# The first matrix of both MLPs by seven block products for the latent tokens, its feature sums made beside the norm

## The chip, the cores and the metric

The kernel runs on 1 core of a Trainium2 chip. The metric is the device time of one execution in microseconds. The core has a matrix engine (PE, with weight loads shown as PEld), a vector engine (DVE), an engine for activations (ACT), a general one (POOL) and SP, which here issues all DMA transfers.

## The reference

One inference step of a backbone of two layers with 1280 tokens: 1024 latent ones and 256 prompt ones, 1024 features each. After a mixer (DeltaNet and attention in the first layer, a gated recurrence in the second) every layer has an MLP with 4096 hidden features:

```
def sq_relu_mlp(h, w1, w2):
    return jnp.square(jax.nn.relu(h @ w1)) @ w2
...
yp = yp + (mp[5] * sq_relu_mlp(modulate(yp, norm2_g[l], mp[3], mp[4]), ff_w1[l], ff_w2[l])).astype(yp.dtype)
ys = ys + (ms[5] * sq_relu_mlp(modulate(ys, norm2_g[l], ms[3], ms[4]), ff_w1[l], ff_w2[l])).astype(ys.dtype)
```

`modulate` is an RMS norm over the features, times a scale per feature, plus a shift per feature. `p` stands for the prompt tokens and `s` for the latent ones; everything is float32.

## The kernel before

Features lie on the partitions, in eight chunks of 128; tokens lie along the free dimension in three groups (`TT`, line 24): group 0 and group 1 are 512 latent tokens each, group 2 is the 256 prompt tokens. Each float32 operand of a large matmul is split into a high part (a cast to the matmul type, on ACT) and a low part (the rest, subtracted on DVE or POOL), and each product is three matmuls (high by high, high by low, low by high; `gemm_tile`, lines 463 to 468). `wload` (439) loads a chunk of weights through raw slots (`wraw`, four of them in the MLPs), and keeps high and low parts in one of four weight slots.

The work around the change runs in this order in each layer.

- `OutProj.finish` (689) multiplies the mixer's result by the output projection, adds it to x (`evac`, line 702, on DVE) and calls `step` after each of the eight output chunks of a token group. First come chunks 0 to 3 for all groups, then chunks 4 to 7 of group 0, of group 1, of group 2. x stays in SBUF in three tiles, `x0` to `x2`.
- `norm_steps` (736) builds the norm into these steps. `Norm.square` (387) squares a chunk on ACT (line 396) and lets PE add up the chunk before it (`flush`, line 332). `stat` (398) turns the sums into 1/rms per token; `apply` (409) scales the chunks on DVE (418), makes the high part on ACT (419) and the low part on DVE (421) or POOL (427). Group 0's `stat` and `apply` are called at steps 4 and 5 of group 1, group 1's at steps 4 and 6 of group 2, and group 2's are left to the first pair of ff1. The squares and the scaled chunks share four scratch slots (`t0` in `ffr`, `t1` in `tt`, two each).
- `ff1` (491) goes over 16 pairs `p` of hidden chunks. For each token group and each chunk of the pair it runs 8 x 3 matmuls, a relu on ACT (506) and a square on DVE (507). Then POOL makes four differences of the hidden blocks (511), and the hidden features and the differences go to DRAM (`Dh`, `Dt`, lines 513 and 514).
- `ff2` (517) goes over eight groups of four hidden chunks. It has the second matrix for the latent tokens as seven block products of a 2 x 2 scheme, from those differences and from sums of weights that POOL makes, and adds each to x (`acc`, line 526).

No order is written out: the framework's planner, at build time, puts the instructions of each engine in order by its own estimates of their costs, and takes among those that are ready the one that comes first in the program. The profile shows matmuls of ff1 between those of OutProj, for instance. At run time each engine keeps to the order it was given.

## Time and profile before

| what | us |
|---|---|
| median of 3 runs | 3238.04 (3234.08 to 3239.82) |
| the profiled execution | 3233.86 |
| its span, first to last instruction | 3232.1 |
| PE busy in the span | 3060.8 |
| DVE, ACT, POOL busy | 1864.1, 1209.4, 1117.5 |

PE's matmuls overlap, so a row's duration (0.39 us for 512 columns) is longer than the distance from one to the next; the rate is read from start to start. Of the stages that the change touches, ff1 runs from some 1092 to 1525 us in the first layer and from some 2397 to 2830 us in the second, each followed by ff2. A wait names the instruction that released the waiting one.

### The profile page before, as it was taken

The page shows a single profiled execution, that of the slowest core. Times are in us where ns is not written, and L with a number is a line of the kernel's source. Part 1 is how long each engine was busy: PE and PEld are TensorE (multiplying, and loading weights), DVE is VectorE, ACT ScalarE, POOL GpSimd, SP SyncE. Part 2 cuts the span into 40 slices and gives each one's busy share as a digit, 9 for nine tenths or more (in the row PEclk, how much of TensorE's full clock was granted, in tenths as well). Part 3 has the DMA queues.
Part 4 walks back from the last instruction along what each step waited for, and adds up shares of the span by engine and source line. Part 5 has one row for each costly group of instructions (what it writes and reads, how often), then busy time and mean ns, then how long its engine had stood idle before and what let it go on. Part 6 is the DMA issues. An engine that isn't in the chain of part 4 may idle for free.

```text
span 3232.1 us, 50272 instructions
## 1 busy us (share of the span) xinstructions
PE 3060.8 (95%) x19927; PEld 2485.3 (77%) x19927; DVE 1864.1 (58%) x2952; ACT 1209.4 (37%) x1972; POOL 1117.5 (35%) x781
## 2 busy tenths in 40 slices
PE   8989975889989999999999998999899999999999
PEld 5776764565557788888888877888678888888888
DVE  5548887576751522223777766888352222277776
ACT  5555433454331411112333335878241111133332
POOL 0000004454531432334767641000133333287664
PEclk9999986999999999999999998999999999999999
DMA  5346677536871233334534230110313333454332
GB/s 205 85 142 175 172 180 188 156 124 208 245 239 52 69 127 127 127 127 170 181 110 157 84 106 24 37 45 25 108 46 139 120 123 119 153 191 149 128 107 85
DMA packets 274058, 416.53 MB, mean 129 GB/s; under 512 B 77210, under 2 KB 139450, under 8 KB 269726
## 3 DMA queue, kind: packets, MB, share of 16 engines
q1 hardware_dynamic: 273822, 413.31, 40.0%
q8 instruction: 157, 2.57, 0.3%
q14 instruction: 79, 0.65, 0.1%
HBM read 290.80 MB, written 122.41 MB: 128 GB/s over the span
## 4 chain that ended last, share of the span: by engine, by line
PE 74%; DVE 8%; DMA 3%; issue 3%; ACT 2%; POOL 2%; SPq 1%; DVEq 0%; POOLq 0%; ACTq 0%
PE ps_mm L467 14%; PE ps_mm L466 14%; PE ps_mm L468 13%; PE ps_w L546 4%; PE ps_w L547 4%; PE ps_w L548 4%; PE ps_mm L547 4%; PE ps_mm L548 4%; PE ps_mm L546 4%; DVE prod L1600 2%; PE ps_ad L300 2%; PE ps_w L1959 1%; DVE Vinv L1601 1%; PE ps_w L1955 1%; PE ps_s L1918 1%
## 5 line engine op out<-in xcount | busy, mean ns | idle before, releaser
L466 PE MATMUL ps_mm<-hhi,whi 128*128 128x512 f32 (+2 forms) x2768 | 991.0, 359 | 24.7 <-ACT hhi L686 13.5
L467 PE MATMUL ps_mm<-hlo,whi 128*128 128x512 f32 (+2 forms) x2768 | 990.2, 358 | 8.8 <-POOL hlo L427 8.8
L468 PE MATMUL ps_mm<-hhi,wlo 128*128 128x512 f32 (+2 forms) x2768 | 987.6, 357 | 1.6 <-POOL wlo L457 1.6
L466 PEld LDWEIGHTS ps_mm<-hhi,whi 128*128 128x128 f32 (+1 forms) x2768 | 525.8, 190 | 111.1 <-ACT hhi L686 13.9
L467 PEld LDWEIGHTS ps_mm<-hlo,whi 128*128 128x128 f32 (+1 forms) x2768 | 526.2, 190 | 90.7 <-POOL hlo L427 11.6
L468 PEld LDWEIGHTS ps_mm<-hhi,wlo 128*128 128x128 f32 (+1 forms) x2768 | 526.3, 190 | 81.8 <-issue 6.0
L507 DVE TENSOR_TENSOR hid<-ffr 128x512 f32<-128x512 f32 (+1 forms) x192 | 148.9, 777 | 589.3 <-ACT ffr L506 507.1
L536 POOL TENSOR_TENSOR wlo<-ar,whi 128x1024 fp32r<-128x1024 f32 x96 | 246.7, 2584 | 268.7 <-ACT whi L535 251.2
L506 ACT ACTIVATE ffr<-ps_mm 128x512 f32<-128x512 f32 (+1 forms) x192 | 100.6, 525 | 548.2 <-PE ps_mm L468 546.5
L526 DVE SCALAR_TENSOR_TENSOR x<-ps_mm,mod,x 128x512 f32<-128x512 f32 x272 | 200.4, 746 | 82.8 <-PE ps_mm L548 82.6
L526 DVE SCALAR_TENSOR_TENSOR x<-ps_w,mod,x 128x512 f32<-128x512 f32 (+1 forms) x304 | 185.6, 632 | 100.7 <-PE ps_w L548 100.5
L511 POOL TENSOR_TENSOR tt<-hid 128x512 f32<-128x512 f32 x64 | 83.3, 1301 | 414.0 <-DVE hid L507 414.0
L453 ACT CAST whi<-wraw 128x512 fp32r<-128x512 f32 (+1 forms) x237 | 136.7, 617 | 197.9 <-PE ps_mm L467 84.1
L535 ACT CAST whi<-ar 128x1024 fp32r<-128x1024 f32 x96 | 98.0, 1051 | 292.6 <-PE ps_w L547 208.3
L457 POOL TENSOR_TENSOR wlo<-wraw,whi 128x512 fp32r<-128x512 f32 (+1 forms) x93 | 139.1, 1515 | 186.1 <-DVE hlo L687 93.0
L828 POOL MEMSET pad<- 128x2 f32 (+2 forms) x60 | 3.9, 119 | 439.8 <-DVE xc L846 200.0
L457 DVE TENSOR_TENSOR wlo<-wraw,whi 128x512 fp32r<-128x512 f32 x144 | 136.2, 972 | 33.2 <-ACT whi L453 33.0
L546 PE MATMUL ps_w<-pp,whi 128*128 128x256 f32 x512 | 143.6, 283 | 4.6 <-DVE x L526 4.6
L547 PE MATMUL ps_w<-pp,whi 128*128 128x256 f32 x512 | 143.4, 283 | 0.0
L548 PE MATMUL ps_w<-pp,wlo 128*128 128x256 f32 x512 | 141.0, 283 | 0.0
L511 POOL TENSOR_TENSOR tt<-hid,tt 128x512 f32<-128x512 f32 x64 | 85.3, 1333 | 118.2 <-DVE hid L507 118.0
L702 DVE SCALAR_TENSOR_TENSOR x<-ps_mm,mod,x 128x512 f32<-128x512 f32 (+1 forms) x40 | 25.9, 655 | 150.3 <-PE ps_mm L468 138.5
(416 smaller groups left out, 5890.1 us busy)
## 6 DMA issues: line engine op xcount, KB each, us to landing
...
wraw<-ff SPq DMA_DIRECT2D x128, 256.0 KB
...
br<-dh SPq DMA_DIRECT2D x128, 256.0 KB
ar<-ff SPq DMA_DIRECT2D x128, 256.0 KB
br<-dt SPq DMA_DIRECT2D x128, 256.0 KB
...
```

The lines of the kernel that those rows point to most:

```text
L453: nc.scalar.copy(hv[:, o:o + half], raw[:, :half])
L457: e.tensor_tensor(lv[:, o:o + half], raw[:, :half], hv[:, o:o + half], op=ALU.subtract)
L466: nc.tensor.matmul(ps, whi[:, k, :], hhi[:, k, :], start=first and k == k0, stop=False)
L467: nc.tensor.matmul(ps, whi[:, k, :], hlo[:, k, :], start=False, stop=False)
L468: nc.tensor.matmul(ps, wlo[:, k, :], hhi[:, k, :], start=False, stop=last and k == k1 - 1)
L507: nc.vector.tensor_tensor(hid[i][:, t0:t0 + tw], r[:, :tw], r[:, :tw], op=ALU.mult)
L511: nc.gpsimd.tensor_tensor(t[:, j], x, y, op=ALU.subtract)
L526: nc.vector.scalar_tensor_tensor(xt[ti][:, o, :], ps[:, :tw], Gt[:, o, cc:cc + 1], xt[ti][:, o, :], op0=ALU.mult, op1=ALU.add)
L536: nc.gpsimd.tensor_tensor(lo[:, c], s, hi[:, c], op=ALU.subtract)
L546: nc.tensor.matmul(ps, ah, bh, start=first, stop=False, skip_group_check=True)
L547: nc.tensor.matmul(ps, ah, bl, start=False, stop=False, skip_group_check=True)
L548: nc.tensor.matmul(ps, al, bh, start=False, stop=last, skip_group_check=True)
```

## The change

For the two groups of latent tokens, a pair of hidden chunks and the two halves of the input features are taken as a 2 x 2 by 2 x 2 block product, made with seven products in place of eight. A product is four feature chunks by three matmuls of 512 columns. The weight sums are made for every pair on POOL, in place, in the raw tiles; their high and low parts take four weight slots per pair instead of two. The feature sums (blocks 2, 3 and 4) are made once per layer, while group 1 is normed; they take the SBUF of the x tiles, so x is stored to DRAM (`Dxm`) during OutProj and loaded again at the start of ff2. The norm of the latent groups now scales x in place, without scratch. Group 2 (prompt) keeps its 2 x 8 x 3 matmuls of 256 columns per pair. The four differences of hidden blocks are made on DVE and stored one by one. All norms send the last chunk's sum to PE in `square` instead of in `stat`, and their scratch is one set of four slots (`ffr`). In ff2, half of the feature blocks take a tile `t4` in place of a second `tt`.

```diff
-        if k == KC - 1 and self.late:
-            self.sq = self.g.cp.tile([128, 512], F32, tag="nsq", name="nsq", bufs=1)[:, :self.tw]
-        else:
-            self.sq = self.al("t%d" % (k % 2))[:, :self.tw]
+        self.sq = self.al("t%d" % (k % 2))[:, :self.tw]
         self.g.nc.scalar.activation(self.sq, self.x[:, k, :], AF.Square)
+        if k == KC - 1:
+            self.flush(k)
     def stat(self):
         g, nc, nch = self.g, self.g.nc, self.nch
-        self.flush(KC - 1)
...
+class NormBlocks(Norm):
+    def scaled(self, k, pb, At):
+        x = self.x[:, k, :]
+        self.g.nc.vector.scalar_tensor_tensor(x, x, At[:, k, 0:1], pb, op0=ALU.mult, op1=ALU.mult)
+        return x
+    def biased(self, hi, lo, t, sh):
+        self.g.nc.scalar.activation(hi, t, AF.Identity, bias=sh)
+        self.g.nc.vector.scalar_tensor_tensor(lo, t, sh, hi, op0=ALU.add, op1=ALU.subtract)
+    def plain(self, hi, lo, t):
+        self.g.nc.scalar.copy(hi, t)
+        self.g.nc.gpsimd.tensor_tensor(lo, t, hi, op=ALU.subtract)
+    def apply(self, At, Bt, hhi, hlo):
+        if self.ti == 2:
+            Norm.apply(self, At, Bt, hhi, hlo)
+            self.last_block()
+            return
+        g, nc, com = self.g, self.g.nc, self.com
+        pb = self.rows()
+        hi, lo = hhi[self.ti], hlo[self.ti]
+        if self.ti == 0:
+            for k in range(KC):
+                self.biased(hi[:, k, :], lo[:, k, :], self.scaled(k, pb, At), Bt[:, k, 0:1])
+            com["x0"] = self.x
+            return
+        dsh = g.cp.tile([128, 4], F32, tag="dsh", name="dsh", bufs=1)
+        nc.vector.tensor_tensor(dsh, Bt[:, 4:8, 0], Bt[:, 0:4, 0], op=ALU.subtract)
+        d2, d3 = [[g.fp.tile([128, 2, 512], F32, tag="hid", name="nd", bufs=4) for i in range(2)] for _ in range(2)]
+        com["d4"] = g.fp.tile([128, 4, 512], F32, tag="tt", name="nd4", bufs=1)
+        x0 = com["x0"]
+        for k in range(4):
+            u, v = self.scaled(k, pb, At), self.scaled(4 + k, pb, At)
+            t, e2, e3 = x0[:, k, :], d2[k // 2][:, k % 2], d3[k // 2][:, k % 2]
+            nc.vector.tensor_tensor(t, u, t, op=ALU.subtract)
+            nc.vector.tensor_tensor(e2, v, t, op=ALU.subtract)
+            nc.gpsimd.tensor_tensor(e3, v, u, op=ALU.subtract)
+            nc.gpsimd.tensor_tensor(com["d4"][:, k], x0[:, 4 + k, :], e2, op=ALU.subtract)
+            self.plain(hi[:, k, :], lo[:, k, :], t)
+            self.biased(hi[:, 4 + k, :], lo[:, 4 + k, :], v, Bt[:, 4 + k, 0:1])
+        for n, (d, tag) in enumerate(((d2, "x0"), (d3, "x1"))):
+            t = g.xm.tile([128, 2, 4, 512], F32R, tag=tag, name=f"tb{2 + n}", bufs=1)
+            for k in range(4):
+                self.biased(t[:, 0, k], t[:, 1, k], d[k // 2][:, k % 2], Bt[:, 4 + k, 0:1] if n == 0 else dsh[:, k:k + 1])
+            com[2 + n] = (t[:, 0], t[:, 1])
+    def last_block(self):
+        g, com = self.g, self.com
+        hi = g.xm.tile([128, 4, 512], F32R, tag="x2", name="tb4h", bufs=1)
+        lo = g.fp.tile([128, 4, 512], F32R, tag="t4", name="tb4l", bufs=1)
+        for k in range(4):
+            self.plain(hi[:, k], lo[:, k], com["d4"][:, k])
+        com[4] = (hi, lo)
...
-def ff(g, l, xt, hhi, hlo, Gt, pend, after):
+def ff(g, l, Dxm, h, com, Gt, pend, after):
     Dh = g.dp.tile([NFC // 2, 128, 2, T], F32, name=f"dh{l}")
     Dt = g.dp.tile([NFC // 2, 128, 4, 512], F32, name=f"dt{l}")
-    ff1(g, l, hhi, hlo, pend, Dh, Dt)
-    ff2(g, l, xt, Gt, after, Dh, Dt)
+    ff1(g, l, h, com, pend, Dh, Dt)
+    xt = [xtile(g, ti) for ti in range(3)]
+    ff2(g, l, xt, Dxm, Gt, lambda o, ti: after(o, ti, xt[ti]), Dh, Dt)
...
+def three(g, ps, a, b, first, last):
+    (ah, al), (bh, bl) = a, b
+    g.nc.tensor.matmul(ps, ah, bh, start=first, stop=False, skip_group_check=True)
+    g.nc.tensor.matmul(ps, ah, bl, start=False, stop=False, skip_group_check=True)
+    g.nc.tensor.matmul(ps, al, bh, start=False, stop=last, skip_group_check=True)
+def wslot(g):
+    w, i = g.wslots[g.nw % len(g.wslots)]
+    g.nw += 1
+    return [w.tile([128, KC, 128], F32R, tag=n + str(i), name=n).rearrange("p k c -> p (k c)") for n in ("whi", "wlo")]
...
+def ff1(g, l, h, com, pend, Dh, Dt):
+    def product(ps, w, half, b, first):
+        for k in range(4):
+            c = slice(512 * half + 128 * k, 512 * half + 128 * k + 128)
+            three(g, ps, [v[:, c] for v in w], [v[:, k, :] for v in b], first and k == 0, k == 3)
+    def saved(ps):
+        t = scratch()
+        nc.scalar.copy(t, ps)
+        return t
+    def square(out, ps):
+        r = scratch()[:, :out.shape[-1]]
+        nc.scalar.activation(r, ps, AF.Relu)
+        nc.vector.tensor_tensor(out, r, r, op=ALU.mult)
+    def add_square(out, t, ps):
+        nc.vector.tensor_tensor(out, t, ps, op=ALU.add)
+        nc.vector.scalar_tensor_tensor(out, out, 0.0, out, op0=ALU.max, op1=ALU.mult)
+    def sum_(out, x, y, op=ALU.subtract):
+        nc.gpsimd.tensor_tensor(out, x, y, op=op)
+    def parts(srcs, e):
+        hi, lo = wslot(g)
+        for j, s in enumerate(srcs):
+            c = slice(512 * j, 512 * j + 512)
+            nc.scalar.copy(hi[:, c], s)
+            e.tensor_tensor(lo[:, c], s, hi[:, c], op=ALU.subtract)
+        return hi, lo
...
+        if p % 2:
+            t = pool.tile([128, 2, 2, 512], F32, tag="tt", name="raw", bufs=1)
+            raw = [[t[:, i, j] for j in range(2)] for i in range(2)]
+        else:
+            raw = [[wraw(g) for j in range(2)] for i in range(2)]
+            for j in range(2):
+                nc.sync.dma_start(raw[i][j], g.A["ff1"][l, 2 * p + i][:, 512 * j:512 * j + 512])
+        (a11, a12), (a21, a22) = raw
+        w1, w2 = parts((a11, a12), nc.gpsimd), parts((a21, a22), nc.vector)
+        sum_(a22, a21, a22, ALU.add)
+        sum_(a21, a11, a21)
+        sum_(a11, a22, a11)
+        sum_(a12, a12, a11)
+        s12, s34 = parts((a22, a11), nc.vector), parts((a21, a12), nc.gpsimd)
+        hid = [pool.tile([128, 1024], F32, tag="hid", name="hid", bufs=4) for i in range(2)]
+        hp = [pool.tile([128, 256], F32, tag="hidp", name="hidp", bufs=2) for i in range(2)]
+        (b11, b12), (b21, b22) = [[t[:, 0:512], t[:, 512:1024]] for t in hid]
+        def prompt(i, w):
+            ps = bank(g, "w")[:, :256]
+            for k in range(KC):
+                three(g, ps, [v[:, 128 * k:128 * k + 128] for v in w], (hhi[2][:, k, :], hlo[2][:, k, :]), k == 0, k == KC - 1)
+            square(hp[i], ps)
+        def late():
+            if pend:
+                pend.pop(0)()
+        ca = bank(g, "mm")
+        product(ca, w1, 0, part(0, 0), True)
+        late()
+        t = saved(ca)
+        ps = bank(g, "w")
+        product(ps, w1, 1, part(0, 4), True)
+        late()
+        add_square(b11, t, ps)
+        if p:
+            prompt(0, w1)
+        product(ca, s12, 1, com[2], False)
+        u1 = saved(ca)
+        cb = bank(g, "w")
+        product(cb, s12, 0, part(1, 0), True)
+        product(ca, s34, 0, com[3], False)
+        u2 = saved(ca)
+        add_square(b22, u2, cb)
+        if not p:
+            prompt(0, w1)
+        prompt(1, w2)
+        product(ca, w2, 1, com[4], False)
+        square(b21, ca)
+        product(cb, s34, 1, part(1, 4), False)
+        add_square(b12, u1, cb)
+        ts = []
+        for j, (x, y) in enumerate(((b12, b11), (b22, 0), (b22, b12), (b21, 1))):
+            ts.append(scratch())
+            nc.vector.tensor_tensor(ts[j], x, ts[y] if j % 2 else y, op=ALU.subtract)
+            nc.sync.dma_start(Dt[p, :, j], ts[j])
+        for i in range(2):
+            nc.sync.dma_start(Dh[p, :, i, 0:NL], hid[i])
+            nc.sync.dma_start(Dh[p, :, i, NL:], hp[i])
...
         chain = [bank(g, "mm") for m in range(4)]
         load_w(0)
         a11, b11 = weights([ar[:, 0]]), feats(block_of(0, 0))
+        if gi == 0:
+            load_x(g, xt[0], xsrc, 0)
...
+        if gi == 0:
+            load_x(g, xt[2], xsrc, 2)
         prompt((a11, a12), 0)
...
         w, f = weights(s2), feats(comb(2))
+        if gi == 0:
+            load_x(g, xt[1], xsrc, 1)
         for m in range(4):
...
-            return g.fp.tile([128, T], F32R, tag="hid", name="ndg", bufs=4)
-        return g.fp.tile([128, 512], F32, tag={"t0": "ffr", "t1": "tt"}[tag], name="n" + tag, bufs=2)
+            return g.fp.tile([128, 1024], F32R, tag="hid", name="ndg", bufs=4)
+        return g.fp.tile([128, 512], F32, tag="ffr", name="n" + tag, bufs=4)
...
-    step, left, h = norm_steps(g, (At, Bt), ff_scratch(g), {1: 4, 2: 4}, {1: 5, 2: 6})
-    xt = op.finish(cut, g.mod[l][:, 16:24, :], step)
-    ff(g, l, xt, *h["h"], Gt, left, lambda o, ti: after(o, ti, xt[ti]))
+    com = {}
+    Dxm = g.dp.tile([128, KC, T], F32, name=f"dxm{l}")
+    step, left, h = norm_steps(g, (At, Bt), ff_scratch(g), {1: 4, 2: 4}, {1: 5, 2: 6}, com=com)
+    def keep(o, ti, x):
+        step(o, ti, x)
+        if o % 4 == 3:
+            t0, tw = TT[ti]
+            nc.sync.dma_start(Dxm[:, o - 3:o + 1, t0:t0 + tw], x[:, o - 3:o + 1, :])
+    op.finish(cut, g.mod[l][:, 16:24, :], keep)
+    ff(g, l, Dxm, h["h"], com, Gt, left, after)
```

## Rows read from the trace of the kernel before

**Rows 1.** The page of the profile, its start and part 1, whole span.

```profile
span 3232.1 us, 50272 instructions
...
PE 3060.8 (95%) x19927; PEld 2485.3 (77%) x19927; DVE 1864.1 (58%) x2952; ACT 1209.4 (37%) x1972; POOL 1117.5 (35%) x781
```

**Rows 2.** Busy time by stretch: ff1 of both layers, ff2 of the first.

```profile
core 0: us, PE busy (x) PEld busy (x) DVE busy (x) ACT busy (x) POOL busy (x), PEclk, DMA share, GB/s
1092.00:1525.00 433.00, 431.89 (x2261) 372.59 (x2261) 125.76 (x147) 89.74 (x171) 138.31 (x101) 1.00 0.36 126
2397.00:2830.00 433.00, 431.89 (x2263) 372.65 (x2263) 125.44 (x147) 89.15 (x170) 139.26 (x101) 1.00 0.36 126
1600.00:1800.00 200.00, 200.00 (x1065) 173.34 (x1065) 148.08 (x178) 65.26 (x72) 133.75 (x70) 1.00 0.38 127
```

**Rows 3.** Timeline of PE, one pair: start us, us, engine, line, operation.

```profile
1302.75 0.40 PE L466 MATMUL ps_mm<-hhi,whi 128*128 128x512 f32 x1
...
1324.54 0.28 PE L466 MATMUL ps_mm<-hhi,whi 128*128 128x256 f32 x1
...
1330.29 0.40 PE L466 MATMUL ps_mm<-hhi,whi 128*128 128x512 f32 x1
```

**Rows 4.** Groups by line and shape inside ff1: count | busy, mean ns | idle before.

```profile
L457 POOL TENSOR_TENSOR wlo<-wraw,whi 128x512 fp32r<-128x512 f32 x28 | 44.1, 1594 | 0.0
...
L511 POOL TENSOR_TENSOR tt<-hid 128x512 f32<-128x512 f32 x30 | 38.8, 1295 | 206.4 <-DVE hid L507 206.4
L507 DVE TENSOR_TENSOR hid<-ffr 128x512 f32<-128x512 f32 x56 | 38.8, 692 | 229.8 <-ACT ffr L506 195.8 <-issue 34.0
L457 DVE TENSOR_TENSOR wlo<-wraw,whi 128x512 fp32r<-128x512 f32 x28 | 37.1, 1364 | 9.5 <-ACT whi L453 9.5
L506 ACT ACTIVATE ffr<-ps_mm 128x512 f32<-128x512 f32 x56 | 33.5, 598 | 256.3 <-PE ps_mm L468 256.3
L453 ACT CAST whi<-wraw 128x512 fp32r<-128x512 f32 x56 | 32.0, 618 | 52.4 <-POOL tt L511 26.4 <-PE ps_mm L467 25.9
```

**Rows 5.** Timeline of DVE from OutProj to ff1, first layer (columns as rows 3).

```profile
1056.98 0.75 DVE L702 SCALAR_TENSOR_TENSOR x<-ps_mm,mod,x 128x512 f32<-128x512 f32 x1 [1.33 <-PE ps_mm L468]
1059.48 0.75 DVE L418 SCALAR_TENSOR_TENSOR nt<-x,A,ps_w 128x512 f32<-128x512 f32 x1 [1.75 <-PE ps_w L369]
...
1072.97 0.47 DVE L702 SCALAR_TENSOR_TENSOR x<-ps_mm,mod,x 128x256 f32<-128x256 f32 x1
...
1081.30 0.16 DVE L403 TENSOR_SCALAR nst<-ps_w 128x4 f32<-128x4 f32 x1 [4.93 <-PE ps_w L347]
...
1084.89 1.41 DVE L418 SCALAR_TENSOR_TENSOR nt<-x,A,ps_w 128x512 f32<-128x512 f32 x2 [1.12 <-PE ps_w L369]
```

**Rows 6.** Waits of PE, 960 to 1120 us: total us, times, longest.

```profile
PE ps_mm L466 <- ACT hhi L419: 2.7, 2, 1.6
PE ps_mm L467 <- POOL hlo L427: 2.3, 1, 2.3
PE ps_w L368 <- DVE ndg L361: 0.9, 1, 0.9
```

**Rows 7.** Busy time by stretch after those waits (columns as rows 2).

```profile
1085.00:1091.00 6.00, 2.28 (x6) 1.55 (x7) 5.96 (x8) 4.30 (x7) 2.94 (x2) 0.68 0.00 0
```

**Rows 8.** Groups by line and shape, whole span: the norm (columns as rows 4).

```profile
L421 DVE SCALAR_TENSOR_TENSOR hlo<-nt,mod,hhi 128x512 fp32r<-128x512 f32 x25 | 28.3, 1138 | 0.2
...
L418 DVE SCALAR_TENSOR_TENSOR nt<-x,A,ps_w 128x512 f32<-128x512 f32 x40 | 27.8, 738 | 6.9 <-PE ps_w L369 6.9
...
L418 DVE SCALAR_TENSOR_TENSOR nt<-x,A,ps_w 128x256 f32<-128x256 f32 x24 | 10.1, 473 | 0.8 <-PE ps_w L369 0.8
...
L421 DVE SCALAR_TENSOR_TENSOR hlo<-nt,mod,hhi 128x256 fp32r<-128x256 f32 x15 | 9.8, 655 | 0.8 <-ACT hhi L419 0.8
```

**Rows 9.** Busy time by stretch: start of ff2; reload of x (columns as rows 2).

```profile
1500.00:1545.00 45.00, 42.82 (x235) 37.08 (x234) 28.40 (x25) 15.20 (x20) 30.80 (x16) 1.00 0.82 290
2280.00:2290.00 10.00, 8.65 (x40) 7.02 (x39) 2.52 (x4) 3.45 (x6) 2.55 (x2) 1.00 1.05 383
```

More of the change, by code (lines that the diff above doesn't have):

```diff
@@ L407, in stat, with rows @@
         self.dg = diag_rows(g, rs, dg[:, :512], dg[:, 512:1024])
+    def rows(self):
+        pb = bank(self.g, "w")[:, :self.tw]
+        spread_rows(self.g, pb, *self.dg)
+        return pb
     def apply(self, At, Bt, hhi, hlo):
@@ L517, in ff2 @@
-def ff2(g, l, xt, Gt, after, Dh, Dt):
+    ff1(g, l, h, com, pend, Dh, Dt)
[6 more added lines that the diff above has]
+    g.nc.tensor.matmul(ps, al, bh, start=False, stop=last, skip_group_check=True)
@@ new lines, in wslot, with part, scratch @@
+def wslot(g):
[3 more added lines that the diff above has]
+def ff1(g, l, h, com, pend, Dh, Dt):
+    nc, pool = g.nc, g.fp
+    hhi, hlo = h
+    def part(ti, k0):
+        return hhi[ti][:, k0:k0 + 4, :], hlo[ti][:, k0:k0 + 4, :]
+    def product(ps, w, half, b, first):
+        for k in range(4):
+            c = slice(512 * half + 128 * k, 512 * half + 128 * k + 128)
+            three(g, ps, [v[:, c] for v in w], [v[:, k, :] for v in b], first and k == 0, k == 3)
+    def scratch():
+        return pool.tile([128, 512], F32, tag="ffr", name="ffr", bufs=4)
+    def saved(ps):
[18 more added lines that the diff above has]
+        return hi, lo
+    for p in range(NFC // 2):
+        if p % 2:
[3 more added lines that the diff above has]
+            raw = [[wraw(g) for j in range(2)] for i in range(2)]
+        for i in range(2):
+            for j in range(2):
[50 more added lines that the diff above has]
+            nc.sync.dma_start(Dh[p, :, i, NL:], hp[i])
@@ L521, in ff2 @@
+def ff2(g, l, xt, xsrc, Gt, after, Dh, Dt):
     nc, pool, src = g.nc, g.fp, g.A["ff2"][l]
@@ L528, in weights @@
     def weights(srcs):
-        w, i = g.wslots[g.nw % len(g.wslots)]
-        g.nw += 1
-        hi, lo = [w.tile([128, KC, 128], F32R, tag=n + str(i), name=n).rearrange("p k c -> p (k c)") for n in ("whi", "wlo")]
+        hi, lo = wslot(g)
         n = 1024 // len(srcs)
@@ L542, in split @@
         return hi, lo
-    def three(ps, a, b, first, last):
-        (ah, al), (bh, bl) = a, b
-        nc.tensor.matmul(ps, ah, bh, start=first, stop=False, skip_group_check=True)
-        nc.tensor.matmul(ps, ah, bl, start=False, stop=False, skip_group_check=True)
-        nc.tensor.matmul(ps, al, bh, start=False, stop=last, skip_group_check=True)
     def product(pss, a, b, m, first):
@@ L552, in product @@
             c, t = slice(512 * i + 128 * m, 512 * i + 128 * m + 128), slice(512 * i, 512 * i + 512)
-            three(pss[m], [v[:, c] for v in a], [v[:, t] for v in b], first and i == 0, i == 1)
+            three(g, pss[m], [v[:, c] for v in a], [v[:, t] for v in b], first and i == 0, i == 1)
     for gi in range(NG):
@@ L572, in feats @@
             if count[0] % 2:
-                t = pool.tile([128, 2, 1024], F32R, tag="tt", name="bb", bufs=2)
+                t = pool.tile([128, 2, 1024], F32R, tag=("tt", "t4")[count[0] // 2 % 2], name="bb", bufs=1)
                 return split(raw, t[:, 0], t[:, 1])
@@ L589, in prompt @@
                         f = 256 * (2 * i + c)
-                        three(ps, [v[:, w] for v in ws[c]], [pp[:, x, f:f + 256] for x in range(2)], i + c == 0, i + c == 2)
+                        three(g, ps, [v[:, w] for v in ws[c]], [pp[:, x, f:f + 256] for x in range(2)], i + c == 0, i + c == 2)
                 acc(ps, 2, o0 + m)
@@ L743, in after @@
         if o == 0:
-            n[ti] = Norm(g, ti, x, al)
-            n[ti].late = i == 2
+            n[ti] = Norm(g, ti, x, al) if com is None else NormBlocks(g, ti, x, al)
+            n[ti].com = com
         n[ti].square(o)
```

23 lines of the change are left out of this document (2 added, 21 removed).

## The prediction

> **What bounds the kernel now.** I read the page's first part, then the busy time by stretch, then one pair of hidden chunks in the timeline. PE is busy 95% of the span, every other engine at most 58% [rows 1]. Inside ff1 PE is busy 431.89 of 433 us in either layer, at granted clock 1.00, with DVE and POOL both under a third [rows 2]: ff1 is matmul-bound, and a matmul taken out there is time. Its pace is in the timeline [rows 3]: from 1302.75 to 1324.54 us lie 96 matmuls of 512 columns (two chunks x two latent groups x eight feature chunks x three), 0.227 us apart; to 1330.29 another 48 of 256 columns, 0.120 us apart. A pair takes 27.54 us, and PE goes into the next without a wait. PE does wait where OutProj hands over to ff1: 5.9 us in the first layer, all on the norm's results [rows 6], and right after it runs at a granted clock of 0.68 [rows 7], part of that stretch at the lower of its two levels (1.2 instead of 2.4 GHz).
>
> **Matmuls removed.** Seven products of 4 x 3 matmuls are 84 of 512 columns in place of 96; the prompt keeps its 48. A pair is then 84 x 0.227 + 48 x 0.120 = 24.82 us, 2.72 us less. There are 16 pairs in 2 layers; the first of each layer is costed with the hand-over below, so 30 x 2.72 = **-81.7 us**. ff2 is already done by seven products here, and in its steady stretch PE was busy 200.00 of 200 us with POOL at 133.75 [rows 2], so this form can keep PE full.
>
> **The side work of a pair** has to fit beside 24.82 us. ACT: 8 casts x 0.618, three saved sums and a relu at 0.598, two small relus at some 0.4: 8.1 us [rows 4]. POOL: 4 low parts and 4 weight sums, 8 x 1.30 alone to 1.59 beside DVE: 10.4 to 12.7 us [rows 4]. DVE: 4 low parts (0.69 alone, 1.36 beside POOL) and 4 feature differences at the same, three additions from PSUM (0.74, as L418 [rows 8]), three and a half multiplications at 0.69: 10 to 16 us [rows 4, 8]. SP issues 12 transfers for 7 and moves the same bytes, under stores that no one in ff1 awaits. All fits, so the sums alone cost nothing. What has little room is one chain: w2's slot is free only after product six; then two casts (1.24), the second low part on DVE (0.69 to 1.36), three POOL sums (3.9 to 4.8), a cast (0.62) and a low part (0.69 to 1.36) before s12 can start product three of the next pair: 7.1 to 9.4 us [rows 4], in 11.0 us of PE work (product seven, two products, one prompt part: 3 x 2.72 + 2.88), or 13.9 if the planner puts the second prompt part first. DVE has the pair's closing work in the same stretch (add-and-square, four differences: 4.2 to 6.9 us). I take 0.4 us of wait per pair, **+12 us**; ends 0 and 2.7 or more.
>
> **Hand-over to ff1.** Today the last 512-token evacuation is at 1056.98, the norm of group 0 starts on DVE at 1059.48, OutProj's last evacuation is at 1072.97, and the norm of group 1 starts only at 1084.89, after its sums at 1081.30 [rows 5]. PE bridges that with group 0's 10.9 us of the first pair. After the change group 0 feeds only 5.4 us (products one and two); product three needs block 2, made of both groups. DVE's list grows: group 0, eight scalings and eight low parts (for five); group 1, eight scalings, eight differences, four low parts, then eight more for blocks 2 and 3: 28 instead of 13. POOL gets twelve for four. Group 0 at 0.70 (two L418 took 1.41 [rows 5]) and 1.14 [rows 8] is 14.7 us, with four evacuations of 0.47 and the statistics some 18: group 1 could start at 1077.6 at the latest. Its squares no longer share two scratch slots with that norm, and the program allows it after OutProj's third prompt step, some 1066; I take 1071. A step of its loop of four is two scalings (1.4), three DVE operations with two SBUF inputs (2.1) and three on POOL (3.9): 3.9 us if both run freely. The rows show a subtract on DVE of 0.69 alone and 1.36 beside POOL, POOL's 1.30 becoming 1.59 [rows 4], so I take 5.0 us, 20 for four. Block 2's first low part is then at 1092, product three ends at 1095.5, block 3 and product five at 1100, the prompt features (8 x 0.47 + 5 x 0.66 [rows 8]) at 1107, both prompt parts and product six at 1112; a clock at half after the idle stretch costs some 2: 1114. Today's first pair ends near 1071 + 27.5 + 5.9 + 2 = 1106.5. So **+7 us** per layer in place of a gain; ends -8.6 (wait gone, 2.72 saved) and +18 (start at 1077.6, a step at 6.0, DVE low parts at 1.14). The second pair is fed late: its w1 slot waits for the first prompt part, its raw weights for the tile that holds block 4: 0 to 6, taken **+2** per layer.
>
> On that step there is a rule. By the Trainium skill (SBUF — State Buffer, Who interferes with whom) a DVE instruction with two SBUF inputs and a GpSimd instruction that reads SBUF exclude each other, the second standing still until the first is done. By that a step would be 2.1 + 3.9 = 6.0 us, 4 us more per layer, and the sum 8 us higher; the row's 1.36 for 0.69 is less than a full turn behind a POOL operation of 1.30.
>
> **Order and sums of squares.** The last flush moves from stat into the last square, onto PE right after the eighth evacuation. PE could wait there for the evacuation on DVE (0.75 [rows 5]) and the square on ACT (some 0.6, as L506 [rows 4]), nine times in all; the planner puts ready matmuls between, as it does today. I take 0, ends -5 and +12.
>
> **x by way of DRAM.** Six stores a layer (5.24 MB) have landed long before the norm overwrites x: group 1's last evacuation is at 1056.98 [rows 5] and its first scaling by my count at 1071, 14 us later, and group 0 has longer. If not, DVE waits for the last megabyte (2.7 us at 383 GB/s), with the evacuations queued behind it. The reload stands on SP behind ff2's first weights and features, and ahead of later ones; the accumulation that needs it stands on DVE ahead of the next features' low parts. At the 383 GB/s of today's reload of x it is 13.7 us, and around ff2's start the DMA engines are already at 0.82 [rows 9]. But block 2 frees its tile 13 us before ff1 ends and the first accumulation for group 1 is due 17 us into ff2. I take **+2 us** per layer; ends 0 and 13.7.
>
> **Sum:** -81.7 + 12 + 14 + 4 + 4 = -47.7. The profiled execution took 3233.9 us (span 3232.1 and 1.8 around it): 3186. The median of the three runs stands 4.2 us above it, which I leave inside the range. About 0.2%, 6.5 us, is what a measurement here tells from no change.
>
> **Rivals.**
> 1. *Weights come late in every pair (slower).* Place: s12 before product three, behind w2, the POOL sums and DVE's closing work. If both low parts queue behind that work the chain is 9.4 + 4.2 to 6.9 = 13.6 to 16.3 us. From 2.0 us of wait per pair (a chain of 13.0 us) nothing is left, since 30 x 2.0 + 22 for the other terms is 82. At 3.7 us of wait per pair: 3233.9 - 81.7 + 111 + 22 = 3285. For: 1.36 us in [rows 4] for a subtract. Against: the spare prompt part, and ff2's full PE at a busier POOL [rows 2]. Chance 0.10.
> 2. *The hand-over costs 18 per layer, DVE and POOL in turn:* 3186 + 22 = 3208. Chance 0.15. The rule of the skill's page named above would alone give 3194; its trace bears it out only in part.
> 3. *The reload holds ff2's start for all its 13.7 us a layer and pairs wait 1 us:* 3186 + 23 + 18 = 3227, with any hand-over loss no change. Chance 0.07.
> 4. *Nothing waits:* 3233.9 - 81.7 - 17.2 = 3135. Chance 0.05.
> That the matmuls aren't fewer can't be: their count is written out.
>
> **Numbers.** The forecast holds 0.63, with 3160 to 3212 as its own range. With rivals 2 and 4 in part, 3156 to 3222 leaves out 0.2. Faster by over 0.2%: the forecast, 2, 4 and a small part of 3, 0.85; same 0.05; slower 0.10.
>
> **What would show it.** Right: matmuls of 512 columns 84 to a pair, pairs 24.8 to 25.3 us apart, PE waits in ff1 on wlo or whi below 15 us in all, a wait on the second group's features of 8 to 15 us at each hand-over, at half clock after it. Wrong: PE waits of over 2 us in each pair on weight parts (rival 1), or long waits on x loads after ff2's start (rival 3).

## Result: slower by 0.7%, and the profile after

The changed kernel took 3259.0 us (median of 4 runs, 3254.0 to 3267.0) against 3236.9 for the kernel before: a ratio of 1.0071, interval 1.0044 to 1.0097. Forecast were 3186, at least 3156 and at most 3222. The profiled execution took 3254.0 us, 20.2 more than that of before.

The page of the changed kernel, against [rows 1]:

```profile
span 3251.1 us, 50543 instructions
PE 3009.4 (93%) x19543; PEld 2411.1 (74%) x19543; DVE 2171.6 (67%) x3278; ACT 1292.5 (40%) x2116; POOL 1286.6 (40%) x861
```

384 matmuls are gone, 12 from each of 32 pairs, as the diff says. At 0.227 us they were 87 us of PE; PE is busy 51 us less, and the span is longer. The rest is in the stretches of [rows 2], in the changed kernel:

```profile
1092.00:1525.00 433.00, 404.10 (x2064) 337.20 (x2065) 260.46 (x288) 130.10 (x241) 221.44 (x142) 0.97 0.36 127
2397.00:2830.00 433.00, 398.58 (x2040) 334.06 (x2041) 265.77 (x293) 128.75 (x238) 221.31 (x142) 0.96 0.35 125
1600.00:1800.00 200.00, 200.00 (x1067) 173.19 (x1067) 148.38 (x179) 66.99 (x74) 133.53 (x69) 1.00 0.38 127
```

ff1, which kept PE at work for 432 of 433 us, now leaves it idle for 29 and 34 of them; in the stretch of ff2 it still never waits. From OutProj's last evacuation to the last accumulation of ff2 (the "MLP" below) the first layer took 855.8 us before and takes 866.3, the second 850.2 and 862.8. Products are numbered as `ff1` writes them: one and two use the weight slot w1, three and four s12 (two of the four weight sums), five and seven s34 (the other two), six w2; "the prompt's rows" are the 1/rms values of its tokens, spread over the partitions by two matmuls (L368, L369) ahead of its scaling. PE's waits in the changed kernel, 1060 to 1545 us:

```profile
PE ps_w L368 <- DVE ndg L361: 29.1, 2, 27.9
PE ps_mm L558 <- DVE wlo L608: 9.5, 14, 2.5
PE ps_mm L556 <- ACT whi L607: 3.5, 1, 3.5
PE ps_mm L556 <- ACT ffr L588: 2.8, 3, 1.5
PE ps_w L556 <- ACT whi L607: 1.4, 1, 1.4
```

There is one wait of 27.9 us at the hand-over, and one of about half a microsecond in nearly every pair on the low part of a weight sum. The timeline of PE in the changed kernel shows the first, and a third thing:

```profile
1075.36 0.27 PE L347 MATMUL ps_w<-con,nt 64*128 64x64 f32 x1
1103.56 0.55 PE L368 MATMUL ps_w<-ndg,onesr 128*128 128x256 f32 x1 [27.93 <-DVE ndg L361]
1103.91 0.41 PE L369 MATMUL ps_w<-ndg,onesr 128*128 128x256 f32 x1
1104.12 0.63 PE L556 MATMUL ps_w<-hhi,whi 128*128 128x512 f32 x1
1104.55 0.63 PE L557 MATMUL ps_w<-hlo,whi 128*128 128x512 f32 x1
...
1302.34 0.40 PE L556 MATMUL ps_w<-hhi,whi 128*128 128x512 f32 x1
1302.57 0.40 PE L557 MATMUL ps_w<-hlo,whi 128*128 128x512 f32 x1
1302.80 0.40 PE L558 MATMUL ps_w<-hhi,wlo 128*128 128x512 f32 x1
1303.03 0.28 PE L556 MATMUL ps_w<-hhi,whi 128*128 128x256 f32 x1
1303.15 0.28 PE L557 MATMUL ps_w<-hlo,whi 128*128 128x256 f32 x1
```

At 1075.36 PE has done products one and two and stops at the spreading of the prompt's norm rows; behind it, at 1104, matmuls follow each other 0.43 us apart: the granted clock from 1104 to 1107 us is 0.50, the lower level. Far from any wait, at full clock, the 512-column matmul comes every 0.23 to 0.235 us (the "pitch"; 233.3 ns in the mean of 1130 to 1290), where before it came every 0.227 [rows 3]; the 256-column one takes 118.3 ns for 120. The same change of pace is in OutProj, which the diff does not touch, and not in ff2's 512-column matmuls. Steady pairs are 26.15 us apart (1226.88 to 1488.37 is ten of them).

DVE in the changed kernel, in the loop over group 1's chunks and in a steady pair:

```profile
1082.68 0.69 DVE L471 TENSOR_TENSOR x<-x,x 128x512 f32<-128x512 f32 x1
1083.28 1.76 DVE L444 SCALAR_TENSOR_TENSOR hlo<-x,mod,hhi 128x512 fp32r<-128x512 f32 x1
1084.96 1.74 DVE L471 TENSOR_TENSOR x<-x,x 128x512 f32<-128x512 f32 x1
...
1351.20 1.78 DVE L668 TENSOR_TENSOR ffr<-hid 128x512 f32<-128x512 f32 x1
1353.01 1.66 DVE L668 TENSOR_TENSOR ffr<-hid,ffr 128x512 f32<-128x512 f32 x1
1354.59 1.77 DVE L668 TENSOR_TENSOR ffr<-hid 128x512 f32<-128x512 f32 x1
1356.29 0.68 DVE L668 TENSOR_TENSOR ffr<-hid,ffr 128x512 f32<-128x512 f32 x1
1356.89 0.68 DVE L608 TENSOR_TENSOR wlo<-raw,whi 128x512 fp32r<-128x512 f32 x1
```

POOL in the same stretches, and ACT in the second:

```profile
1082.63 3.53 POOL L473 TENSOR_TENSOR nd<-x 128x512 f32<-128x512 f32 x2
...
1347.16 5.27 POOL L601 TENSOR_TENSOR raw<-raw 128x512 f32<-128x512 f32 x3 [1.48 <-DVE wlo L608]
```

```profile
1352.46 0.63 ACT L607 CAST whi<-raw 128x512 fp32r<-128x512 f32 x1 [1.08 <-POOL raw L601]
1355.36 0.59 ACT L588 COPY ffr<-ps_mm 128x512 f32<-128x512 f32 x1 [2.28 <-DMA dt<-ffr]
```

Beside POOL a DVE subtract takes 1.74 us in place of 0.69, and POOL's 1.76: one of each every 1.67 to 1.75 us. In the pair, s12's second high part is cast by 1353.1, but its low part starts on DVE at 1356.89, behind all four differences of the pair before. And the copy of product one (L588) waits for a scratch slot until the store of the first difference has left it.

### The profile page after: what moved, and what is told of

It reads as the page before. It is cut to its first block, busy times and chain, and to the rows that moved or that the text cites. A ratio compares the mean times of both kernels' runs of the same rounds, so it can differ in the third digit from the quotient of the medians.

```text
span 3251.1 us, 50543 instructions
## 1 busy us (share of the span) xinstructions
PE 3009.4 (93%) x19543; PEld 2411.1 (74%) x19543; DVE 2171.6 (67%) x3278; ACT 1292.5 (40%) x2116; POOL 1286.6 (40%) x861
## 4 chain that ended last, share of the span: by engine, by line
PE 62%; DVE 16%; issue 7%; DMA 4%; ACT 2%; POOL 2%; SPq 1%; DVEq 0%; ACTq 0%; POOLq 0%
PE ps_w L556 7%; PE ps_w L557 7%; PE ps_w L558 7%; PE ps_mm L558 6%; PE ps_mm L556 6%; PE ps_mm L557 6%; PE ps_mm L528 4%; PE ps_mm L529 4%; PE ps_mm L530 4%; DVE ffr L668 2%; DVE prod L1765 2%; PE ps_ad L300 2%; DVE NI L1732 1%; DVE Vinv L1766 1%; DMA ar<-ff 1%
## 5 line engine op out<-in xcount | busy, mean ns | idle before, releaser
L528 PE MATMUL ps_mm<-hhi,whi 128*128 128x512 f32 (+2 forms) x1232 | 447.3, 364 | 19.1 <-ACT hhi L842 13.4
L529 PE MATMUL ps_mm<-hlo,whi 128*128 128x512 f32 (+2 forms) x1232 | 444.9, 362 | 5.2 <-POOL hlo L429 5.2
L530 PE MATMUL ps_mm<-hhi,wlo 128*128 128x512 f32 (+2 forms) x1232 | 444.3, 362 | 1.4 <-POOL wlo L519 1.4
L556 PE MATMUL ps_w<-hhi,whi 128*128 128x256 f32 (+1 forms) x896 | 297.9, 333 | 3.2 <-ACT whi L607 3.2
L557 PE MATMUL ps_w<-hlo,whi 128*128 128x256 f32 (+1 forms) x896 | 296.6, 333 | 0.0
L558 PE MATMUL ps_w<-hhi,wlo 128*128 128x256 f32 (+1 forms) x896 | 293.3, 333 | 0.0
L528 PEld LDWEIGHTS ps_mm<-hhi,whi 128*128 128x128 f32 (+1 forms) x1232 | 232.8, 189 | 66.8 <-ACT hhi L842 13.8
L529 PEld LDWEIGHTS ps_mm<-hlo,whi 128*128 128x128 f32 (+1 forms) x1232 | 232.6, 189 | 47.4 <-POOL hlo L429 6.5
L530 PEld LDWEIGHTS ps_mm<-hhi,wlo 128*128 128x128 f32 (+1 forms) x1232 | 233.0, 189 | 43.5 <-issue 5.8
L691 ACT CAST whi<-ar 128x1024 fp32r<-128x1024 f32 x96 | 97.8, 1048 | 277.3 <-PE ps_w L557 207.6
L556 PEld LDWEIGHTS ps_w<-hhi,whi 128*128 128x128 f32 x896 | 170.8, 191 | 24.8 <-ACT whi L607 4.0
L588 ACT COPY ffr<-ps_mm 128x512 f32<-128x512 f32 x96 | 56.4, 587 | 324.0 <-PE ps_mm L558 243.6
```

Source lines behind the costliest of these rows:

```text
L528: nc.tensor.matmul(ps, whi[:, k, :], hhi[:, k, :], start=first and k == k0, stop=False)
L529: nc.tensor.matmul(ps, whi[:, k, :], hlo[:, k, :], start=False, stop=False)
L530: nc.tensor.matmul(ps, wlo[:, k, :], hhi[:, k, :], start=False, stop=last and k == k1 - 1)
L556: g.nc.tensor.matmul(ps, ah, bh, start=first, stop=False, skip_group_check=True)
L557: g.nc.tensor.matmul(ps, ah, bl, start=False, stop=False, skip_group_check=True)
L558: g.nc.tensor.matmul(ps, al, bh, start=False, stop=last, skip_group_check=True)
```

## Experiments

The theory after the traces: three losses. (1) The pace of the matmuls. (2) The hand-over, by the order of the work or by DVE's and POOL's sum. (3) The wait in each pair, by DVE's order. Ratios are to the kernel before; MLP times are of the first and the second layer.

### 1. The pace: where tiles lie in SBUF

The removed tile `nsq` (2048 bytes) and the new `dsh` (16, padded to 32) stand ahead of the weight slots. Features are laid out from the other end and did not move. So weights and scratch start 224 bytes into a 256-byte stretch before, as the features do, and 0 bytes in after. Three runs put a tile of n columns of four bytes ahead of the weight slots (n is 24 in a1_shift96, 8 in a2_before32, 56 in b2_shift224):

```diff
+    shift = g.cp.tile([128, n], F32, name="shift")
+    nc.gpsimd.memset(shift, 0.0)
     g.wp = es.enter_context(tile_pool(g, "wp"))
```

> The changed kernel with 96 bytes per partition put ahead of the weight slots in SBUF, nothing else. In the kernel before, weights, scratch and features all begin 96 bytes into a 128-byte line; in the changed one the new 16-byte tile of shift differences (dsh) pushes weights and scratch to 0 while the features, laid out from the other end, stay at 96. Address theory: a matmul whose weights and moving operand stand differently in their 128-byte lines is slower, so here the 512-column pitch in OutProj and ff1 falls back from 233.5 to 226.7 ns and the 256-column one goes from 118.4 to 120; 84 x 6.8 - 48 x 1.6 ns = 0.50 us for each of 32 pairs, 0.29 for each of 16 + 16 projection chunks, -25 us in all: 3234. Rival (the pace comes from what DVE, POOL and DMA do beside PE): pitch stays 233, time 3259 within 3.

> The kernel before with 32 bytes per partition put ahead of the weight slots, nothing else: weights and scratch at 0 in their 128-byte lines, features at 96, as in the changed kernel. Address theory: 512-column pitch 233 ns where the features move against weights (OutProj, ff1, the second mixer's in-projection), 227 in ff2, whose features lie on the weights' side; 96 x 6.8 - 48 x 1.6 ns = 0.58 us for each of 32 pairs, 0.29 for 32 chunks: +28 us, 3265. Rival: 3237 within 3, pitch 227 throughout.

```diff
-    g.neghalf = g.cp.tile([128, 20], F32, name="neghalf")
+    g.neghalf = g.cp.tile([128, 24], F32, name="neghalf")
...
-        dsh = g.cp.tile([128, 4], F32, tag="dsh", name="dsh", bufs=1)
+        dsh = g.neghalf[:, 20:24]
```

> The changed kernel with its 16-byte tile dsh put into the unused end of the tile of exponents (neghalf), so that weights and scratch begin 32 bytes lower: 20960, which is 480 bytes into a 512-byte stretch, as the features are, and as both were in the kernel before. The kernel before moved by 32 bytes took the 232/235 ns pitch of the changed kernel and lost 17 us; the changed kernel moved by 96 bytes (same place in a 128-byte line, another in 512 bytes) did not get it back (228 to 241 ns). Theory now (equal place in a longer stretch than 128 bytes is what counts): 226.7 and 120 ns everywhere, about 0.5 us less in each pair, 3259 - 17 to 25 = 3238. Rival (something else in the changed kernel slows PE): 232 ns stays, 3259 within 3.

> The changed kernel with 224 bytes ahead of the weight slots: weights and features at the same place in a 256-byte stretch, 256 bytes apart in one of 512. If 256 bytes is the period, the 512-column pitch in ff1 is 226.7 ns; if it is 512 or more, it stays above 229.

| run | start of weights, of features, modulo 256 | 512-column pitch in ff1, ns | us | ratio |
|---|---|---|---|---|
| before | 224, 224 | 226 to 227 | 3236.9 | 1 |
| after | 0, 224 | 231 to 235 | 3259.0 | 1.0071 (1.0044 to 1.0097) |
| a2_before32 | 0, 224 | 231 to 235 | 3255.1 | 1.0050 (1.0034 to 1.0066) |
| a1_shift96 | 96, 224 | 228 to 241 | 3263.7 | 1.0076 (1.0061 to 1.0090) |
| b1_dsh | 224, 224 | 226 to 227, some to 236 | 3254.0 | 1.0051 (1.0037 to 1.0065) |
| b2_shift224 | 224, 224 (256 apart in 512) | as b1_dsh | 3254.0, one run | |

PE in a2_before32, the kernel before with 32 bytes more in front (against [rows 3]):

```profile
1251.65 0.40 PE L469 MATMUL ps_mm<-hlo,whi 128*128 128x512 f32 x1
1251.88 0.40 PE L470 MATMUL ps_mm<-hhi,wlo 128*128 128x512 f32 x1
1252.12 0.40 PE L468 MATMUL ps_mm<-hhi,whi 128*128 128x512 f32 x1
1252.35 0.40 PE L469 MATMUL ps_mm<-hlo,whi 128*128 128x512 f32 x1
```

32 bytes slow the kernel before by 17 us, with the same two distances, 0.23 and 0.235: the pace hangs on where weights and moving operand start against each other, and equal places modulo 256 give the fast one (a1's 128 was a wrong guess at the period). It is not the weights' own place: in ff2 of the changed kernel the latent features lie on the weights' side, both start at 0, and the pitch stays at 227 ns. 28 us were expected; the MLPs lost 7.5 and 8.9 us of the 9.3 worked out for each, the projections less than thought. In the changed kernel the cure gives 5 us of the 17 to 25 expected, and not even these are clear of noise, as the intervals of `after` and b1_dsh overlap; in the two profiled executions the MLPs differ by 0.7 and 1.0. The cured version's pitch is 228.3 ns in the mean, which shortens PE's own work by some 0.4 us a pair, but its steady pairs are 25.88 us apart for 26.15: the wait in each has grown by 0.1. Why became clear in 3.

### 2. The hand-over: order, or DVE and POOL

```diff
         product(ca, w1, 0, part(0, 0), True)
-        late()
...
         product(cb, s12, 0, part(1, 0), True)
+        late()
         product(ca, s34, 0, com[3], False)
+        late()
```

> The changed kernel; the two steps of the prompt's norm are issued behind products four and five of the first pair instead of behind one and two. Order theory (PE stood at the prompt's row spreading, 27.9 us in each layer, with products four and three ready behind it): the wait begins at the same place but ends when group one's first block is split, about 20 us after, and the products then follow as blocks come; 6 to 10 us less in each layer, 3243. Chain theory (DVE and POOL take turns through the whole hand-over, the same work has to be done by them before the first pair can end): the 27.9 us split into several waits, the first pair ends within 3 us of today's, 3259 within 5.

3274.4 us, 1.0105 (1.0086 to 1.0125): the chain theory, and worse than it expected. The one wait became nine of 0.7 to 6.7 us; products four, three and five ran early, but the prompt's norm rows came 46.7 us after the last evacuation for 36.4, with its 48 matmuls of the first pair behind them, to 1135.1 us. MLP 873.8 and 871.0.

```diff
-            nc.gpsimd.tensor_tensor(e3, v, u, op=ALU.subtract)
-            nc.gpsimd.tensor_tensor(com["d4"][:, k], x0[:, 4 + k, :], e2, op=ALU.subtract)
-            self.plain(hi[:, k, :], lo[:, k, :], t)
+            nc.scalar.copy(e3, v)
+            nc.scalar.copy(com["d4"][:, k], x0[:, 4 + k, :])
+            nc.scalar.copy(hi[:, k, :], t)
+            nc.scalar.copy(lo[:, k, :], t)
```

> As b1_dsh, and in the loop over the chunks of group one POOL does nothing: the differences e3 and d4 and the low part of block one, three POOL operations a chunk, are left out (ScalarE copies stand in their places, so blocks one, three and four hold other numbers). Turn theory (a DVE operation with two SBUF inputs and a POOL operation run one after the other, 1.67 us for both against 0.69 for DVE's alone): the loop of 21.5 us takes 14 to 15, the wait of 27.9 us before the prompt's rows is 6 to 8 shorter in each layer. Rival (DVE's twenty operations and their waits on ACT set the loop): DVE's durations go back but the loop stays above 20 us.

3225.5 us in its one run. The kernel leaves out POOL's three operations a chunk, so its results are other numbers. DVE in b4_noport, then PE's longest wait at its hand-over:

```profile
1084.45 0.69 DVE L471 TENSOR_TENSOR x<-x,x 128x512 f32<-128x512 f32 x1
1085.06 0.74 DVE L444 SCALAR_TENSOR_TENSOR hlo<-x,mod,hhi 128x512 fp32r<-128x512 f32 x1
1085.72 0.68 DVE L471 TENSOR_TENSOR x<-x,x 128x512 f32<-128x512 f32 x1
...
1091.34 0.75 DVE L444 SCALAR_TENSOR_TENSOR tb<-nd,mod,tb 128x512 fp32r<-128x512 f32 x1 [1.06 <-ACT tb L443]
```

```profile
PE ps_mm L557 <- ACT tb L443: 13.9, 1, 13.9
```

With POOL out of the loop the same DVE operations take 0.69 and 0.74 us for 1.74 and 1.76, the loop takes 13.0 us for 21.3, the longest wait is half as long, and the MLPs take 855.3 and 849.1 us, 10.3 and 12.7 under b1_dsh. The turns are shown as what sets the loop. Not all of the gain need be theirs: the loop is 8 us shorter, where 6 to 8 were expected in all, and the planner also put block 2's low parts (1091.34, above) ahead of the prompt's rows. What that order gave was not taken alone. The Trainium skill (SBUF — State Buffer, Who interferes with whom) has such pairs of instructions exclude each other; the trace agrees nearly: one of each in 1.67 to 1.75 us, a little under the 1.98 of 0.69 and POOL's 1.29 in sum.

### 3. The pair: DVE's order, slots, or PE's order

a3_diff holds the differences behind s12's second low part in the next pair (`low`):

```diff
-            nc.vector.tensor_tensor(ts[j], x, ts[y] if j % 2 else y, op=ALU.subtract)
...
+                bi = nc.vector.tensor_tensor(ts[j], x, ts[y] if j % 2 else y, op=ALU.subtract)
+                if low and j == 0:
+                    order(g, bi, low)
```

> The changed kernel; the four differences of a pair (DVE, L668) are held behind the second low part of the next pair's weight sum s12, which today stands behind them. Theory of the wait in each pair: PE's wait on wlo (17.9 us, 26 times) goes, pairs 25.6 us apart at the present pitch, 30 x 0.7 = -20 us: 3239. Rival (DVE and POOL are short in sum in this stretch, the wait only moves to another product, to a scratch buffer or to the stores): pairs stay at 26.1, 3259 within 4.

3343.0 us, 1.0320 (1.0302 to 1.0339), slower by 84 us than the changed kernel. The wait on wlo is gone, and PE in a3_diff waits for product one's copy, 1140 to 1500 us:

```profile
PE ps_mm L556 <- ACT ffr L588: 30.9, 12, 3.3
```

Later differences are stored later, so their scratch slots come free later. b3_pool left the differences alone:

```diff
-        s12, s34 = parts((a22, a11), nc.vector), parts((a21, a12), nc.gpsimd)
+        s12, s34 = parts((a22, a11), (V, P)), parts((a21, a12), (P, P))
```

> As b1_dsh, and the second low part of the weight sum s12 is made by POOL right behind the sum it comes from, instead of by DVE behind the four differences. Theory (PE's wait at product three is for this one operation in DVE's order): the wait on wlo of 17.9 us goes to under 5, pairs 25.0 us apart, 30 x 0.6 = 18 us below b1_dsh, about 3220. Rival (POOL's own chain of sums and low parts is as late): the wait comes back at product five, on s34's low part, and the time is b1_dsh's within 4.

3377.3 us, 1.0430 (1.0415 to 1.0444): neither theory's number. Differences run beside POOL again and the planner set the queues anew; waits on whi, on ffr and on hid of 1 to 2 us, several a pair, at a granted clock of 0.94. What of it came first was not followed.

The next four runs build on b1_dsh. c1_early and e1_slotsonly are two edits alone, d1_slots has both, and e2_diffslots joins the second with a3_diff's. Early w2 (w2 is also split ahead of w1, and the prompt's hidden features are stored as each is made):

```diff
+        if p:
+            prompt(1, w2)
+            cc = bank(g, "mm")
+            product(cc, w2, 1, com[4], True)
         ca = bank(g, "mm")
         product(ca, w1, 0, part(0, 0), True)
...
+            add_square(b21, u2, cc)
```

Named slots (`t` has slot 0, `u1` 1, `u2` 2; squares are made in place, and the norms' scratch goes round the same four names):

```diff
-        return pool.tile([128, 512], F32, tag="ffr", name="ffr", bufs=4)
+        return pool.tile([128, 512], F32, tag=f"ffr{i}", name="ffr", bufs=1)
...
-        nc.scalar.activation(r, ps, AF.Relu)
-        nc.vector.tensor_tensor(out, r, r, op=ALU.mult)
+        nc.scalar.activation(out, ps, AF.Relu)
+        nc.vector.tensor_tensor(out, out, out, op=ALU.mult)
...
-            ts.append(scratch())
+            ts.append(scratch((3, 2, 1, 3)[j]))
```

> As b1_dsh, and in each pair but the first the two products of w2 (the prompt's and product six, in a PSUM bank of its own, added to u2 afterwards) stand ahead of product one. w2's slot then comes free 5.6 us into a pair instead of 2.7 before its end, so the chain w2, sums, s12 begins some 17 us earlier against product three. Theory (the pair's length is set by this chain from slot to slot, PE's own work being 84 x 226.7 + 48 x 120 ns = 24.8 us): no wait on wlo, pairs 24.8 to 25.1 us apart instead of 25.9, 30 x 0.9 = 27 us below b1_dsh: 3227. Rival (scratch buffers and the stores behind the differences are as late, as in the two trials before): waits on ffr in its place, 3254 within 4 or slower.

> As c1_early, with the four scratch buffers of ff1 given by name instead of in turn: the copy of product one has one to itself (in turn it came to stand behind the first difference's store, 3.1 us from its making to its slot's release), the squares are made in place and take none. Theory (in c1_early the wait moved from s12 to this slot): no wait on ffr, PE's own work sets the pair: 24.8 to 25.0 us apart, ff1 444 us in each layer against 458.6 in b1_dsh, 3254 - 29 = 3225. Rival (DVE, POOL and the stores are short in sum, a third wait comes): pairs 26 or more, above 3250.

> As b1_dsh, with the named scratch buffers and the squares in place of d1_slots, but w2's products where they were. If the chain from w2's slot to s12 sets the pair by itself, the wait on wlo stays, pairs about 25.9 us apart, 3254 within 4, and both edits were needed. If the scratch slots alone held it, pairs of 25.0 and 3214 to 3220.

> As e1_slotsonly, and the four differences held behind the second low part of s12, as in a3_diff. There the wait on wlo went and waits on ffr came; with a scratch buffer of its own for the copy of product one these should go too. If DVE's order and the slots are all that was wrong, pairs of 25.0 us and 3214 to 3222; if the chain from w2's slot is too long even in the best order (two casts, a low part, three POOL sums at 1.3 to 1.7, a cast, a low part: 8 to 10 us in 11.0 of PE work), a wait of up to 0.5 us stays, 3222 to 3240.

| run | edits on b1_dsh | matmuls in 1250 to 1450 us | MLP, us | us | ratio |
|---|---|---|---|---|---|
| b1_dsh | none | 1019 | 865.6, 861.8 | 3254.0 | 1.0051 |
| c1_early | early w2 | 967 | 886.1, 878.8 | 3287.2 | 1.0155 (1.0136 to 1.0174) |
| e1_slotsonly | slots | 1014 | 875.6, 866.2 | 3268.2 | 1.0106 (1.0077 to 1.0135) |
| e2_diffslots | slots, differences behind s12 | 1061 | 859.9, 850.8 | 3236.9 | 1.0004 (0.9991 to 1.0016) |
| d1_slots | slots, early w2 | 1064 | 846.9, 840.3 | 3213.8 | 0.9927 (0.9913 to 0.9940) |

What holds c1_early is in ACT's row at the top of a pair and in PE's longest sum of waits behind the hand-over's, what holds e1_slotsonly in PE's waits (both 1060 to 1560 us):

```profile
1234.06 0.38 ACT L593 ACTIVATE ffr<-ps_w 128x256 f32<-128x256 f32 x1 [6.21 <-DMA dt<-ffr]
```

```profile
PE ps_w L556 <- ACT ffr L593: 16.8, 11, 2.7
```

```profile
PE ps_mm L558 <- DVE wlo L607: 15.6, 15, 2.7
```

With w2 early alone PE waits for scratch, with scratch free alone it waits for s12: each cure alone shows the other illness, and either alone is slower than none. Why e1_slotsonly is 14 us above b1_dsh, with pairs only 0.2 us longer, was followed no further. With the slots free, DVE's order alone (e2) is enough for a full PE in that window, so the chain from w2's slot does fit into its 11.0 us. Its time is still 15 us above the 3222 that this was to give at most. Early w2 saves more: from 1490 to 1545 us, where ff1 ends, PE waits 8.5 us in e2 and 2.9 in d1, and the granted clock is 0.88 and 1.00, worth up to 6.6 of the 55 us. Together that is up to 12.2 of the 13.0 us between their first layers. d1_slots, from its page and then its window 1250 to 1450:

```profile
PE 2988.2 (93%) x19543; PEld 2417.8 (75%) x19543; DVE 2119.1 (66%) x3308; ACT 1274.4 (40%) x2086; POOL 1237.6 (39%) x861
```

```profile
1250.00:1450.00 200.00, 200.00 (x1064) 173.10 (x1063) 111.34 (x146) 56.67 (x106) 87.96 (x65) 1.00 0.40 138
```

132 matmuls a pair at 1064 in 200 us are 24.8 us: the matmul price of the forecast, and a version that beats both kernels.

> As d1_slots, with dsh a tile of its own again: weights and scratch 32 bytes higher, out of step with the features. Address theory, where PE's own work sets the pair: 84 x 6.8 - 48 x 1.6 ns = 0.50 us a pair, 15 us in both layers, and 2 to 5 in the projections: 17 to 20 us above d1_slots. If the pair is set by a chain beside PE, as in the changed kernel, 5 us.

3227.4 us, 0.9971 (0.9957 to 0.9985), 13.6 above d1_slots, 17 to 20 expected. Its window 1250 to 1450 holds 1048 matmuls, 25.2 us a pair. Where PE's own work sets the pair, the 32 bytes cost nearly what they cost the kernel before; in the changed kernel, where the chain sets it, 5 at most.

c2_o021 is c1_early with the prompt ahead of group one:

```diff
-        for ti in range(3):
+        for ti in (0, 2, 1):
             for o in range(4, KC):
                 run([(o, ti)])
```

> As c1_early, and the out-projection ends with group one instead of the prompt: the prompt's features are made before group one's, and the prompt's two products of the first pair (5.8 us each) stand behind products one and two, where PE waits 27.9 us today; group one's norm begins some 8 us later. Theory (PE has no work in the hand-over that does not hang on group one): the prompt's 11.5 us fill part of the wait, against 3 to 5 us from the later start, 6 to 8 us less in each layer: 3214. Rival (the end of DVE's and POOL's work, not PE's, ends the first pair): within 4 of c1_early.

3289.7 us, 1.0164 (1.0144 to 1.0185), as c1_early: the rival. (The expectation priced the prompt's products too high: 48 matmuls of 0.120 us are 5.8 us for the two at full clock, not for each.) They fill part of the gap, and PE then waits 8.2 and 4.6 us for block 2, which comes later. MLP 886.9 and 873.9, 0.8 above and 4.9 below c1_early's.

## Why the prediction was wrong

**Matmuls removed, -81.7.** The count was right. The price was right only for PE: 24.82 us a pair is what d1_slots does. In the changed kernel the pace itself was lost, 84 x 6.4 - 48 x 1.5 ns = 0.5 us a pair; that all the side work "fits, so the sums alone cost nothing" had no line for a tile's address, and a 16-byte tile in the diff was read past. Alone this explains little of the time: b1_dsh takes it back and is not clearly faster.

**The pair's wait, +12 (0.4 us a pair).** The chain was the right one and 7.1 to 9.4 us in 11.0 the right size: e2_diffslots runs it with PE busy for 200.00 of 200 us. What failed is its last clause, that DVE's closing work, named with its 4.2 to 6.9 us, would add only 0.4. The planner put all of it ahead of s12's low part, in turn with POOL at 1.7 us each. Not seen was the second hold behind it: four scratch slots in turn, in which product one's copy follows the differences' stores. Steady pairs were 26.15 us apart where 25.22 were forecast: 14 us a layer over fifteen, some 7 of them pace and 7 wait; ff1's last microseconds (1506 to 1523) waited some 6 more.

**Hand-over, +7 a layer.** The loop's start (1075.5 for 1071) and its step (21.3 us for four, 5.3 for 5.0) were nearly right. By the rule of the Trainium skill (SBUF — State Buffer, Who interferes with whom) the step would have been 6.0; the trace lies between. The 1.36 us that spoke against a full turn was the mean of two kinds: of the 28 subtracts on line 457 in the kernel before, 14 took 1.77 to 1.78 us and 13 took 0.96 to 0.99 (min/median/max below), and the 0.69 beside it was the square of line 507.

```profile
L457 DVE TENSOR_TENSOR wlo<-wraw,whi x28: 679/1380/1778, 1116.5 to 1469.6; 128x512 fp32r<-128x512 f32 x28
```

What failed is the sequence laid behind it, block 2 at 1092, product three at 1095.5: block 2's low parts ran at 1109.4 to 1112.8, behind the prompt's rows and most of its features, and PE stood at the prompt's row spreading (DVE in the changed kernel, then PE in the kernel before, where the third pair starts):

```profile
1109.41 3.43 DVE L444 SCALAR_TENSOR_TENSOR tb<-nd,mod,tb 128x512 fp32r<-128x512 f32 x4
```

```profile
1137.51 0.40 PE L466 MATMUL ps_mm<-hhi,whi 128*128 128x512 f32 x1
```

Product seven of the first pair ends at 1126.3, 59.1 us after the last evacuation at 1067.2; forecast were 41. The 33.5 for the kernel before was too low as well: less one pair of 27.54, its third pair's start leaves 1110.0 for the end of the first, 37.0 us after its last evacuation at 1073.0. So the hand-over cost 22 us where 7 were forecast. The first pair's 31 us of matmuls and 28 of wait did not overlap. The two reorderings tried did not cure it (a4_late, c2_o021); b4_noport, with less work for POOL and another order, did (10 and 13 us). The list of DVE's work also lacked the first pair's own weight parts, 8 POOL and 4 DVE operations in the same stretch.

**Order and sums of squares, 0; x by way of DRAM, +2 a layer.** OutProj's evacuations spanned 88.7 us for 89.1 in the first layer. From ff2's first accumulation to its last it took 402.9 and 401.2 us for 401.4 and 395.8, and PE's only wait on an accumulation was 0.6 us. No run took these parts alone.

**The sum.** The MLPs missed by 34 and 37 us (forecast -47.7 / 2 = -23.9 in each layer, measured +10.5 and +12.6): as read in the first layer, 15 in the first pair, 14 in the other fifteen, and the rest mostly where ff1 ends. The 68 us between 3186 and 3254 are these 71, less what the stages ahead of and between them happened to gain.

**The rivals.** Rival 2 was near the hand-over's price (18 a layer, measured 22) and rival 1 the mechanism in the pairs (s12 behind DVE's closing work, at some 1 us a pair, not 3.7). Both held at once. They were costed one at a time, each against a forecast that was otherwise right, and the range up to 3222 left out rivals 1 and 3, which reach 3285 and 3227; 3259 lies between. The signposts worked: waits on wlo and whi came to 14.4 us in the first layer alone, and the hand-over's wait to 27.9 for 8 to 15.
